# Order of the last two blocks, gather rate, return of inputs and a table load in a hybrid block with PEER

## The chip, the cores and the metric

The kernel runs on 1 core of one Trainium2 chip. The metric is the device time of one execution in microseconds (us), 2298.05 as the median of 3 runs of the kernel before (2295.23 to 2303.24).

## The reference

One layer, 256 tokens of width 2048, all in float32. A modulated RMS norm of x feeds one projection w_in, whose columns go to a spatial-gating MLP and to a retention of 8 heads; two gated projections of these are added, multiplied by w_o, scaled by a gate and added to x. Then comes PEER: from the second normed and modulated h2, 8 heads choose 16 of 128 x 128 experts per token; each expert has a row u and a row v of 2048 values. What is computed in the part that matters here:

```
a = einsum('td,thkd->thk', xt, emb_u[it])
w = gelu(a) * gate
y = einsum('thk,thkd->td', w, emb_v[it])
x = x + ga2 * y
out = rmsnorm(x, norm_f_g)
```

## The kernel before, in words

The program is one long list of instructions, written with a planner that gives each engine its order: of what is ready by its own model it takes first what stands first in the program, and adds the semaphore waits. A tile pool with n buffers makes the next writer wait until the last reader of that buffer is done.

The stages up to PEER's choice are jobs, each a weight matrix streamed in 1 MB tiles on SP's queue, split into a high and a low part (ScalarE casts the high part, line 213; VectorE subtracts, line 215), and multiplied on TensorE (line 414). The w_o jobs are the last before the second norm. After each of their eight 256-column pieces, `wo_post` (line 661) adds the result to x, takes sums of squares on ScalarE (line 675) and stores x1 to device memory. `norm2` (line 715) then reduces the sums, takes reciprocal and square root (`rsqrt`, lines 169 to 172) and starts the choice of experts on TensorE behind `prs` (line 723).

The last stage computes y. Columns 0 to 575 of each chosen row of peer_v are gathered, one DMA for each of 256 (token half, choice) pairs (`fly`, line 1100, issued by GpSimd at line 757 and spread over the products), and VectorE weighs and adds them into yg (`weigh`, line 1103). The other 1472 columns come as a product: all weights stand in a table A of 128 x 128 experts per token, and each of NK = 128 blocks multiplies a 128 x 256 slice of A by 128 rows of peer_v. `v_load` (line 1116) loads a block's rows vb on SP's queue (three buffers), casts the slice to wh and vb to vh on ScalarE, and subtracts to wl and vl on VectorE (two buffers each). A block is 18 products, (wh, vh), (wl, vh), (wh, vl) for 2 token halves and 3 chunks of 512, 512 and 448 columns. All six sums stay in PSUM through the stage.

The loop (line 1184) runs over blocks 0 to 125. After the products of a block it issues gathers at `rate` per block, 256 / (NK - ENDS), weighs all but BEHIND = 4 of those in flight, and after block BACK it calls `restore`, which loads ga2, x1 and norm_f_g (four loads of 1024 KB) into a part of A that is no longer read. Each of these loads waits for the last product of that block. The two last blocks are multiplied after the loop, one token half at a time; each half ends in `finish` (line 1160): `residual` multiplies a chunk by ga2, adds x1 and squares (the gathered columns' part on GpSimd and ScalarE), then the sums are reduced, the root is taken, the chunks are scaled and stored. The residual's first multiplication also waits for the last vl.

Of the kernel before, what the change touches and what calls it, by code (L numbers as in the profile page):

```python
# [10 lines left out]
F32 = mybir.dt.float32  # L11
# [11 lines left out]
P = 128  # L23
T = 256
TT = T // P
# [8 lines left out]
NK = 128  # L34
# [26 lines left out]
FK = KD - UK  # L61
GW = 576
ON_POOL = ((0, 3), (1, 3))
BACK, ENDS = NK - 5, 4
VG, BEHIND, BEHIND_U = 7, 4, 2
COLS = 2 * NK - 50
GV = D - GW
# [49 lines left out]
def block_kernel(ctx, tc, a, out):  # L117
    nc = tc.nc
    def pool(name, side, bufs=1, space=None):
        stack = ExitStack()  # L120
        kw = {} if space == bass.MemoryType.DRAM else {"reuse_waits": "tile"}
        if space is not None:
            kw["space"] = space
        return stack.enter_context(tc.tile_pool(name=name, bufs=bufs, side=side, **kw)), stack
# [5 lines left out]
    late = {}  # L130
# [3 lines left out]
    sb, sb_s = pool("p1", "left")  # L134
# [5 lines left out]
    def bank(name):  # L140
        return late["side"].tile([P, 512], F32, tag="side", name=name)
# [32 lines left out]
    ss = sb.tile([P, TT], F32, name="ss")  # L174
# [486 lines left out]
    def wo_post(c, off=0):  # L661
        def post(ps):
            c0 = c * GC
            if c == 0:
                late["x1T"] = st.tile([P, KD, T], F32, tag="A16", name="x1T")
                late["ss"] = sb.tile([P, TT, 8], F32, name="ss2")
            ga, gg = late["ga"][:, off:off + GC], late["gg"][:, off:off + GC]
            xc = st.tile([P, TT, GC], F32, tag="tmp_a", name="xc")
            nc.sync.dma_start(xc, xv[:, :, c0:c0 + GC])
            mx = st.tile([P, TT, GC], F32, tag="tmp_c", name="mx")  # L670
            for tt in range(TT):
                nc.vector.tensor_tensor(mx[:, tt], ps[tt], ga, op=ALU.mult)
            nc.vector.tensor_tensor(xc, xc, mx, op=ALU.add)
            for tt in range(TT):
                nc.scalar.activation(mx[:, tt], xc[:, tt], AF.Square, accum_out=late["ss"][:, tt, c:c + 1])
            nc.sync.dma_start(x1d[:, :, c0:c0 + GC], xc)
            if c0 >= UG:
                hr = st.tile([P, TT, GC], F32, tag="tmp_d", name="x1g")
            else:
                hr = h2b[:, :, c0:c0 + GC]  # L680
            nc.vector.tensor_tensor(hr, xc, gg[:, None, :].to_broadcast([P, TT, GC]), op=ALU.mult)
            if c < 7:
                yield
            pt = bank("pt")
            ptv = pt.rearrange("p (k t) -> p k t", k=2)
            for k in range(2):
                for tt in range(TT):
                    nc.tensor.transpose(ptv[:, k, tt * P:(tt + 1) * P], hr[:, tt, k * P:(k + 1) * P], ident)
            nc.scalar.copy(late["x1T"][:, 2 * c:2 * c + 2], ptv)
        return post  # L690
# [374 lines left out]
    for u in range(-LEAD, units + LAG):  # L1065
        if 0 <= u < units and u % half == 0:
            tt = u // half
# [45 lines left out]
    chunks = [(c, min(512, GV - c)) for c in range(0, GV, 512)]  # L1113
    yp = [[py.tile([P, 512], F32, name=f"yp{tt}_{c}") for c, _ in chunks] for tt in range(TT)]

    def v_load(i):
        room, bufs = (p3, 1) if i % 3 == 2 else (pv, 2)
        vb = room.tile([P, GV], F32, tag="vb", bufs=bufs, name="vb")
        nc.sync.dma_start(vb, v_cols[i * P:(i + 1) * P])
        wh = p3.tile([P, T], F32R, tag="wh", bufs=3, name="wh")  # L1120
        w = of_key(i)
        nc.scalar.copy(wh.rearrange("p (g s) -> p g s", s=2), w)  # L1122
        wl = p3.tile([P, T], F32R, tag="wl", bufs=3, name="wl")
        nc.vector.tensor_tensor(wl.rearrange("p (g s) -> p g s", s=2), w, wh.bitcast(F32).rearrange("p (g s) -> p g s", s=2), op=ALU.subtract)  # L1124
        vh = p3.tile([P, GV], F32R, tag="vh", bufs=2, name="vh")
        nc.scalar.copy(vh, vb)  # L1126
        vl = p3.tile([P, GV], F32R, tag="vl", bufs=2, name="vl")
        late["split"] = nc.vector.tensor_tensor(vl, vb, vh.bitcast(F32), op=ALU.subtract)  # L1128
        return vh, vl, wh, wl
# [30 lines left out]
    def finish(tt):  # L1160
        for m in range(len(chunks)):
            residual(tt, m)
        r = rf[:, tt:tt + 1]
        nc.vector.tensor_reduce(r, ss3[:, tt], axis=AX.X, op=ALU.add)
        rsqrt(r, r, 1.0 / D)
        for c, w, n in parts:
            xs = xo[:, tt, c:c + w]
            if n is None:
                nc.scalar.activation(xs, xs, AF.Copy, scale=r)
            else:  # L1170
                nc.vector.scalar_tensor_tensor(xs, xs, r, gf[:, c:c + w], op0=ALU.mult, op1=ALU.mult)  # L1171
            nc.sync.dma_start(ov[:, tt, c:c + w], xs)

    def product(i, ops, j, tt, n):
        vh, vl, wh, wl = ops
        l, r = ((wh, vh), (wl, vh), (wh, vl))[j]
        c, w = chunks[n]
        return nc.tensor.matmul(yp[tt][n][:, :w], l[:, tt * P:(tt + 1) * P], r[:, c:c + w],  # L1178
                                start=(i == 0 and j == 0), stop=(i == NK - 1 and j == 2))
# [4 lines left out]
    for i in range(NK - 2):  # L1184
        ops = nxt
# [12 lines left out]
    ends = [nxt, v_load(NK - 1)]  # L1198
# [2 lines left out]
    for tt in range(TT):  # L1201
        residual(tt, len(parts) - 1)
    for tt in range(TT):
        for j in range(3):
            for n in range(len(chunks)):
                product(NK - 2, ends[0], j, tt, n)
        for n in range(len(chunks)):
            for j in range(3):
                product(NK - 1, ends[1], j, tt, n)
        finish(tt)  # L1210
    big_s.close()
    p3_s.close()
# [52 lines left out]
```

## Time and profile before

| | |
|---|---|
| median of the runs | 2298.05 us |
| profiled execution: its own time, span | 2299.92 us, 2298.1 us |
| mean granted TensorE clock | 0.980 |
| busy, share of span: TensorE, VectorE, ScalarE, GpSimd | 93%, 78%, 43%, 41% |
| read from device memory, mean rate | 631.59 MB, 278 GB/s |
| last stage's first product, last product, end | 1745.6, 2279.1, 2298.1 us |

PE is TensorE's products, PEld its weight loads, DVE VectorE, ACT ScalarE, POOL GpSimd, SP the queue of most loads; L1178 is line 1178. In a timeline a line has start and length in us, engine, line, operation, output<-input, count, and in brackets the idle time before it and what ended that. A line of windows has the stretch, its length, the busy us (and count) of PE, PEld, DVE, ACT and POOL, the granted clock, the busy share of the DMA engines and what they moved in GB/s. A group has busy us and mean ns, then the idle us before its instructions and what ended them.

### The profile page before, as it was taken

The page shows a single profiled execution, that of the slowest core. Times are in us where ns is not written, and L with a number is a line of the kernel's source. Part 1 is how long each engine was busy: PE and PEld are TensorE (multiplying, and loading weights), DVE is VectorE, ACT ScalarE, POOL GpSimd, SP SyncE. Part 2 cuts the span into 40 slices and gives each one's busy share as a digit, 9 for nine tenths or more (in the row PEclk, how much of TensorE's full clock was granted, in tenths as well). Part 3 has the DMA queues.
Part 4 walks back from the last instruction along what each step waited for, and adds up shares of the span by engine and source line. Part 5 has one row for each costly group of instructions (what it writes and reads, how often), then busy time and mean ns, then how long its engine had stood idle before and what let it go on. Part 6 is the DMA issues. An engine that isn't in the chain of part 4 may idle for free. (4 is left out here: it accounts for less than half of the span.)

```text
span 2298.1 us, 37147 instructions
## 1 busy us (share of the span) xinstructions
PE 2145.9 (93%) x13918; PEld 1921.9 (84%) x13918; DVE 1792.4 (78%) x3402; ACT 999.1 (43%) x1426; POOL 941.3 (41%) x750
## 2 busy tenths in 40 slices
PE   5999999999999998989699999997889999999996
PEld 3678888999999977978599999997888878888785
DVE  3469888888889855688677777778997788888887
ACT  3235556553344445110234444446775444444443
POOL 0000000000000001566634444447896888888784
PEclk9999999999999999999899999998999999999998
DMA  8987777788878866658999999994105999999997
GB/s 337 378 313 268 286 280 280 278 288 292 297 280 296 312 206 216 232 180 276 313 301 321 327 319 322 315 318 128 60 2 187 325 327 336 338 322 331 319 327 272
DMA packets 144311, 638.25 MB, mean 278 GB/s; under 512 B 20721, under 2 KB 26625, under 8 KB 112001
## 3 DMA queue, kind: packets, MB, share of 16 engines
q1 hardware_dynamic: 102146, 459.65, 56.1%
q0 software_dynamic: 41984, 176.23, 22.3%
q8 instruction: 109, 1.79, 0.3%
q14 instruction: 72, 0.59, 0.1%
HBM read 631.59 MB, written 4.20 MB: 277 GB/s over the span
## 5 line engine op out<-in xcount | busy, mean ns | idle before, releaser
L757 POOL DMA_INDIRECT gat<-in_peer_v_rows,eidx x256 | 416.0, 1625 | 106.8 <-issue 38.0
L757 POOL DMA_INDIRECT gat<-in_peer_u_rows,eidx x256 | 312.2, 1220 | 281.7 <-PE mmu L900 178.2
L213 ACT CAST whi<-wt 128x2048 fp32r<-128x2048 f32 x130 | 248.1, 1909 | 280.1 <-PE mm L414 210.1
L764 DVE SCALAR_TENSOR_TENSOR gat<-gat,h2b 128x768 f32<-128x768 f32 x256 | 250.3, 980 | 112.3 <-DMA gat<-in_peer_u_rows,eidx 105.8
L215 DVE TENSOR_TENSOR wlo<-wt,whi 128x2048 fp32r<-128x2048 f32 (+1 forms) x130 | 292.3, 2249 | 52.7 <-ACT whi L213 49.1
L358 POOL DMA_DIRECT2D br<-in_b_ada x32 | 15.8, 495 | 764.7 <-DVE ada_acc L359 719.1
L900 PE MATMUL mmu<-h2T,uhi 128*128 128x256 f32 x2220 | 308.8, 287 | 11.1 <-ACT uhi L711 11.1
L1126 ACT CAST vh<-vb 128x1472 fp32r<-128x1472 f32 x128 | 183.1, 1430 | 300.0 <-DMA vb<-in_peer_v_cols 195.1
L711 ACT CAST uhi<-ub 128x640 fp32r<-128x640 f32 x222 | 161.0, 728 | 317.7 <-DMA ub<-in_peer_u_cols 258.1
L900 PEld LDWEIGHTS mmu<-h2T,uhi 128*128 128x128 f32 x2220 | 285.8, 194 | 15.5 <-ACT uhi L711 15.1
L1109 DVE SCALAR_TENSOR_TENSOR yg<-gat,wrow,yg 128x576 f32<-128x576 f32 x254 | 207.6, 817 | 77.6 <-DMA gat<-in_peer_v_rows,eidx 74.5
L355 DVE SCALAR_TENSOR_TENSOR ada_acc<-wa,sc_col,ada_acc 128x256 f32<-128x256 f32 x480 | 231.8, 483 | 11.5
L1128 DVE TENSOR_TENSOR vl<-vb,vh 128x1472 fp32r<-128x1472 f32 x128 | 215.7, 1685 | 10.4 <-ACT vh L1126 10.4
L1178 PE MATMUL yp<-vl,wh 128*128 128x512 f32 (+1 forms) x768 | 195.5, 389 | 13.7 <-DVE vl L1128 13.4
L900 PE MATMUL mmu<-h2T,ulo 128*128 128x256 f32 x1110 | 175.2, 289 | 24.8 <-DVE ulo L712 22.6
L1178 PE MATMUL yp<-vh,wh 128*128 128x512 f32 (+1 forms) x768 | 192.5, 385 | 3.0 <-ACT wh L1122 2.3
L712 DVE TENSOR_TENSOR ulo<-ub,uhi 128x640 fp32r<-128x640 f32 x222 | 180.4, 823 | 17.5 <-ACT uhi L711 14.1
L1178 PE MATMUL yp<-vh,wl 128*128 128x512 f32 (+1 forms) x768 | 192.6, 385 | 0.0
L1178 PEld LDWEIGHTS yp<-vl,wh 128*128 128x128 f32 x768 | 142.8, 189 | 48.2 <-DVE vl L1128 22.8
L414 PE MATMUL mm<-whi,hT 128*128 128x512 f32 (+1 forms) x832 | 181.8, 363 | 0.0
L900 PEld LDWEIGHTS mmu<-h2T,ulo 128*128 128x128 f32 x1110 | 150.8, 194 | 31.5 <-DVE ulo L712 27.1
L1178 PEld LDWEIGHTS yp<-vh,wh 128*128 128x128 f32 x768 | 144.9, 189 | 28.8 <-ACT wh L1122 2.5
(276 smaller groups left out, 3662.7 us busy)
## 6 DMA issues: line engine op xcount, KB each, us to landing
wa<-in_w_ada SPq DMA_DIRECT2D x96, 1024.0 KB
vb<-in_peer_v_cols SPq DMA_DIRECT2D x128, 736.0 KB
ub<-in_peer_u_cols SPq DMA_DIRECT2D x256, 320.0 KB
wt<-in_w_vg SPq DMA_DIRECT2D x32, 1024.0 KB
wt<-in_w_branch_gate SPq DMA_DIRECT2D x32, 1024.0 KB
wt<-in_w_u SPq DMA_DIRECT2D x16, 1024.0 KB
wt<-in_w_b_out SPq DMA_DIRECT2D x16, 1024.0 KB
wt<-in_w_o SPq DMA_DIRECT2D x16, 1024.0 KB
```

The lines of the kernel that those rows point to most:

```text
L213: nc.scalar.copy(hi, wt)
L215: nc.vector.tensor_tensor(lo[:, :cut], wt[:, :cut], hi[:, :cut].bitcast(F32), op=ALU.subtract)
L355: nc.vector.scalar_tensor_tensor(acc, wt[:, k], s, acc, op0=ALU.mult, op1=ALU.add)
L414: nc.tensor.matmul(job.ps[b], l, r, start=(first and k == 0 and i == 0 and not lo_part), stop=(last and k == job.rows - 1 and lo_part == 1))
L712: late["lo"] = (nc.gpsimd if n < POOL else nc.vector).tensor_tensor(lo[:, :w], ub[:, :w], hi[:, :w].bitcast(F32), op=ALU.subtract)
L757: d = nc.gpsimd.indirect_dma_start(out=g, out_offset=None, in_=table, in_offset=bass.IndirectOffsetOnAxis(ap=rows_of("idx")[:, tt, n:n + 1 ...
L764: return nc.vector.scalar_tensor_tensor(g, g, 1.0, h2b[:, tt, :UG], op0=ALU.mult, op1=ALU.mult, accum_out=pe["wrow"][:, tt, n:n + 1])
L900: mm = nc.tensor.matmul(acc, w[:, k - k0], x, start=(first and k == 0 and i == 0), stop=(last and k == FK - 1 and i == len(steps) - 1))
L1109: d = nc.vector.scalar_tensor_tensor(yg[:, tt], g, w, yg[:, tt], op0=ALU.mult, op1=ALU.add)
L1126: nc.scalar.copy(vh, vb)
L1128: late["split"] = nc.vector.tensor_tensor(vl, vb, vh.bitcast(F32), op=ALU.subtract)
L1178: return nc.tensor.matmul(yp[tt][n][:, :w], l[:, tt * P:(tt + 1) * P], r[:, c:c + w], start=(i == 0 and j == 0), stop=(i == NK - 1 and j = ...
```

## The change

Four edits. BACK goes from block 123 to block 112, ENDS from 4 to 7. In the w_o stage a square root of one column of the sums, whose result nothing reads, is taken after the third piece. The two last blocks are multiplied chunk by chunk: of a chunk first block 126's three products, then block 127's.

```diff
-BACK, ENDS = NK - 5, 4
+BACK, ENDS = NK - 16, 7
@@ wo_post
+            if c == 2:
+                warm = sb.tile([P, TT], F32, name="warm")
+                nc.scalar.sqrt(warm, late["ss"][:, :, 0])
@@ after the loop
     for tt in range(TT):
-        for j in range(3):
-            for n in range(len(chunks)):
-                product(NK - 2, ends[0], j, tt, n)
         for n in range(len(chunks)):
-            for j in range(3):
-                product(NK - 1, ends[1], j, tt, n)
+            for i, ops in enumerate(ends):
+                for j in range(3):
+                    product(NK - 2 + i, ops, j, tt, n)
         finish(tt)
```

## Rows read from the trace of the kernel before

**Rows 1.** Chain that ended last, in order of time (start, length, what), end of run.
```profile
2265.08 14.71 DMA A<-in_norm_f_g
```
**Rows 2.** Windows: a stretch of the last stage, and the loads' last stretch.
```profile
2160.00:2200.00 40.00, 40.00 (x184) 34.10 (x183) 33.44 (x39) 16.25 (x21) 29.49 (x20) 1.00 0.92 317
2264.00:2278.00 14.00, 12.34 (x55) 9.88 (x54) 11.36 (x14) 3.95 (x5) 1.70 (x1) 1.00 0.99 397
```
**Rows 3.** Timeline, TensorE in the last stage: idle places, and products after one.
```profile
1745.58 1.83 PE L1178 MATMUL yp<-vh,wh 128*128 128x512 f32 x6 [2.31 <-ACT wh L1122]
...
1819.17 1.60 PE L1178 MATMUL yp<-vl,wh 128*128 128x512 f32 x6 [1.14 <-DVE vl L1128]
...
2143.95 2.82 PE L1178 MATMUL yp<-vl,wh 128*128 128x512 f32 x6 [3.48 <-DVE vl L1128]
2146.57 2.65 PE L1178 MATMUL yp<-vh,wh 128*128 128x512 f32 x6
...
2150.62 1.48 PE L1178 MATMUL yp<-vl,wh 128*128 128x512 f32 x6
...
2211.23 1.60 PE L1178 MATMUL yp<-vl,wh 128*128 128x512 f32 x6 [0.80 <-DVE vl L1128]
...
2235.63 1.60 PE L1178 MATMUL yp<-vl,wh 128*128 128x512 f32 x6 [0.37 <-DVE vl L1128]
```
**Rows 4.** Groups of GpSimd and VectorE, 1760 to 2260 us.
```profile
L757 POOL DMA_INDIRECT gat<-in_peer_v_rows,eidx x249 | 407.9, 1638 | 93.3 <-issue 36.4 <-PE yp L1178 24.1 <-DVE wl L1124 22.4
L1128 DVE TENSOR_TENSOR vl<-vb,vh 128x1472 fp32r<-128x1472 f32 x121 | 203.9, 1685 | 0.7 <-ACT vh L1126 0.7
L1109 DVE SCALAR_TENSOR_TENSOR yg<-gat,wrow,yg 128x576 f32<-128x576 f32 x247 | 201.4, 815 | 76.4 <-DMA gat<-in_peer_v_rows,eidx 73.3 <-issue 2.4
```
**Rows 5.** Timeline, loads on SP, casts of vb, TensorE's last block.
```profile
2186.46 1.43 ACT L1126 CAST vh<-vb 128x1472 fp32r<-128x1472 f32 x1 [2.22 <-PE yp L1178]
...
2263.20 0.33 SPq L1119 DMA_DIRECT2D vb<-in_peer_v_cols  x1
2263.58 0.43 SPq L1142 DMA_DIRECT2D A<-ga2d  x1
...
2270.11 1.42 ACT L1126 CAST vh<-vb 128x1472 fp32r<-128x1472 f32 x1 [2.52 <-DMA vb<-in_peer_v_cols]
2271.59 0.50 PE L1178 MATMUL yp<-vh,wh 128*128 128x512 f32 x1 [0.67 <-ACT vh L1126]
...
2273.32 0.50 PE L1178 MATMUL yp<-vl,wh 128*128 128x512 f32 x1 [0.99 <-DVE vl L1128]
...
2278.73 0.36 PE L1178 MATMUL yp<-vl,wh 128*128 128x448 f32 x1
```
**Rows 6.** Timeline, VectorE in the last 27 us.
```profile
2271.57 1.69 DVE L1128 TENSOR_TENSOR vl<-vb,vh 128x1472 fp32r<-128x1472 f32 x1 [2.23 <-ACT vh L1126]
...
2281.56 2.49 DVE L1155 TENSOR_TENSOR A<-A 128x448 f32<-128x448 f32 x2
...
2286.55 0.16 DVE L1164 TENSOR_REDUCE rf<-ss 128x1 f32<-128x4 f32 x1 [1.90 <-ACT A L1156]
...
2291.57 2.01 DVE L1171 SCALAR_TENSOR_TENSOR A<-A,rf 128x512 f32<-128x512 f32 x3 [0.27 <-ACT rf L172]
```
**Rows 7.** Timeline, a gap of ScalarE in the w_o stage; then norm2.
```profile
850.84 1.91 ACT L213 CAST whi<-wt 128x2048 fp32r<-128x2048 f32 x1 [2.62 <-issue]
...
905.33 1.09 PE L688 MATMUL pt<-kst,x1g 128*128 128x128 f32 x4 [5.64 <-DVE x1g L681]
905.48 1.28 ACT L172 ACT_TABLE_LOAD   x1
...
905.90 0.17 DVE L171 RECIPROCAL ssum<-ssum 128x2 f32<-128x2 f32 x1
...
906.77 0.20 ACT L172 ACTIVATE ssum<-ssum 128x2 f32<-128x2 f32 x1
...
907.03 1.22 PE L723 MATMUL prs<-kst,ssum 128*128 128x128 f32 x4 [0.61 <-ACT ssum L172]
```

## The prediction

> **What bounds the kernel now.** I read the chain of waits first, for the end of the run: its last long link before the finish is the transfer of norm_f_g, from 2265.08 to 2279.8 us, for which GpSimd waits with its work on the output [rows 1]. The last product ends at 2278.73 + 0.36 = 2279.1 us [rows 5]; the span ends at 2298.1. So 19.0 us pass after TensorE has done its last work, and edits to the end compete for those 19. The windows came second: in the stage of peer_v, TensorE is busy for all of a 40 us stretch while the DMA engines are busy for 92% of it [rows 2]. Third, TensorE's own idle places there: the largest of some 17 between 1760 and 2265 us are waits for vl, the low half of an operand that VectorE computes [rows 3]. Fourth, the groups of GpSimd and VectorE in 1760 to 2260: the 249 gathers of that stretch cost GpSimd 407.9 us of busy time and 36.4 us of fixed idle time, and VectorE waits 73.3 us for gathered rows that it weighs, in order, ahead of the next vl [rows 4]. So three things run close to full beside TensorE: transfers, gather issue, VectorE's order. A block of 18 products takes 3 x 1.32 = 3.96 us when nothing waits (the groups of six follow each other by 1.32 us); 128 of them are 507 us, and the stage takes 2279.1 - 1745.6 [rows 3] = 533.5.
>
> **The square root's table.** In norm2 the table load runs from 905.48 to 906.77, the square root follows at once, and its reader on TensorE starts at 907.03 [rows 7]. The reciprocal ends at 905.90 + 0.17 = 906.07, and TensorE's transposes ahead of that reader end at 905.33 + 1.09 = 906.42. With the table there, the reader starts at 906.42 instead of 907.03: -0.6 us. The added pair in the w_o stage is a load of 1.28 and an operation of 0.20 on ScalarE; it reads sums of squares that are long there. It is hidden by ScalarE's waits in that stage, 2.62 us in the one shown [rows 7]. If it falls just ahead of a split cast instead, the cast and TensorE behind it can be late by 1.5. Range -0.6 to +1.5; I take -0.6, since later squares and copies run under the same table (the final stage does so with only one load).
> The Trainium skill (ScalarE: Activation LUTs, section What ACT_TABLE_LOAD costs) gives the load the same 1283 ns but adds a drain of about 1380 ns per switch. Here no such drain shows: the operation stands directly behind the load [rows 7]. By the page this edit would give about -2.0 and the sum would be 1.4 us lower.
>
> **Gathers end 7 blocks ahead.** The rate goes from 256/124 = 2.065 to 256/121 = 2.116 gathers a block. By the loop's rule a block issues three gathers, not two, at blocks 0, 15, 31, 46, 62, 77, 93 and 108 now, and at 14 blocks then: six more. Three blocks behind each of the seven later ones TensorE waits for vl: 1.14 us at 1819.17, 3.48 at 2143.95, 0.80 at 2211.23 [rows 3], and between these 0.87, 0.76, 0.77 and 1.05; the median is 0.87. After the wait of 3.48 the clock also fell to half: six products begun at 2146.57 took 2.65 instead of 1.48 us [rows 3], and the 18 from 2143.95 ended 2.6 later than at full clock. Six more waits at 0.87 are 5.2; the three further blocks without gathers give back some 0.2 each, and some of the small waits would merge. I take +4. Bounds: -1 (waits come from elsewhere) to +10 (each as dear as the mean, 1.27, plus its share of clock loss). GpSimd leaves little room: (407.9 + 36.4) / 249 = 1.78 us a gather, 3.77 a block at 2.116, of 3.96.
>
> **The inputs return at block 112.** restore issues four transfers of 1024 KB, 4.19 MB, on SP's queue. Now they stand behind the last vb load (2263.20, then 2263.58) [rows 5], when gathers have all but ended: nothing but the tail waits for them. Then they stand between the loads of blocks 116 and 117, with gathers still flowing until block 120. Queued behind them on SP are the vb loads of all later blocks, and behind those vh, vl and the products. At the rate of the stretch in which they run now, 397 GB/s [rows 2], they take 10.6 us. Against that stand: the 8% of DMA time that is free, 1 us over the 12 us that loaded operands last; and the lead that a load has where nothing waits. A load lands 6.9 us after issue (2263.20 to 2270.11 [rows 5]) and is wanted three blocks less about 1.3 us after it, 10.6, so the lead is up to 3.7. That leaves a TensorE wait of 6 us at block 117, and one such wait costs the clock as at 2143.95: +2.6. The waits that this stretch has now go: 0.37 at 2235.63 [rows 3] and 0.67 + 0.99 for the last block's vh and vl [rows 5], -2.0. Net +6.6. Bounds: a wait of 0 (DMA engines take it beside the rest) to 11 (no lead).
>
> **The last two blocks, chunk by chunk.** The same 36 products, 7.9 us. With today's arrival of vl the new order would wait earlier, since the first chunk needs both blocks: +1.4. But the last seven blocks carry no gathers, so vb, vh and vl of block 127 come as soon as their buffers are free, when block 125 ends; I cost this at 0. The order gives VectorE its first finished chunk 6 products into the pair.
> The tail, from TensorE's end E: now 19.0. VectorE needs from the end of its last vl (2271.57 + 1.69) to its last scaling (2291.57 + 2.01) 20.3 us [rows 6]. Of this go the last four weighings of gathered rows, 3.2 (815 ns each [rows 4]), the wait of 1.90 for squares that stood behind GpSimd's work on norm_f_g, and 1.3 by which two additions beside GpSimd took longer (2.49 for two) [rows 6]: 13.9 are left. Its last vl then ends at E - 7.9 + 1.7 = E - 6.2, so its last scaling ends at E + 7.7, and the outputs follow in 4.5 as now (2293.6 to 2298.1): E + 12.2. The tail shrinks by 6.8. Bounds: -9.4, where only the last chunk's own chain counts (multiply, add, square, root, three scalings and output, 9.6), and -4, if VectorE's order is no better.
>
> **Sum.** -0.6 + 4 + 6.6 - 6.8 = +3.2. The profiled execution took 2299.9 with a span of 2298.1, 1.9 over the median of 2298.05; from the median the forecast is **2301 us**. What is won in the tail is spent ahead of it.
>
> **Rivals.** First, the return is hidden: with the lead, and large packets for which the DMA engines go up to 397 GB/s where they otherwise stand near 317 [rows 2], no vb load is late. For it: there are stretches, from 2150 to 2191 all of one, in which each vh waits for TensorE and not for a landing; the cast at 2186.46 stands for 11 [rows 5]. Against: at 2270.11 a load lands too late even with few gathers [rows 5]. Then -0.6 + 1.5 (gathers, near their lower bound) + 0 - 2.0 - 8 (tail, between its bounds) = -9: 2289.
> Second, on the slower side: the return blocks the queue in full. Gathers keep taking their part of the engines while TensorE uses up blocks 113 to 116, so the load of block 117 lands 11 us late, whatever lead there was, and the denser gathers cost 6: -0.6 + 6 + 11 + 2.6 - 2.0 - 6.8 = +10: 2308. It decides from a TensorE wait of over 9 us at block 117. The busy share of 92% speaks for it, the stretches without any landing wait against it.
> The Trainium skill (DMA: Bandwidth & Descriptors, Queues, rings and completion order) says that each DMA engine takes turns between the queues with work, a packet at a time, and serves one queue in order; by that the gathers, on GpSimd's queue, pass the returned inputs while the vb loads, on SP's, cannot. That is this second rival, and no row here has both at once.
> Third, the change doesn't do what it says: the planner puts the return later in SP's order, or the residual's first part late in VectorE's, and the tail stays: -0.6 + 4 - 1 = +2: 2300.
>
> **How the numbers follow.** Forecast case 0.36, hidden 0.34, blocked 0.26, third 0.04. What a measurement can tell from no change is 0.3%, 6.9 us: 2291.2 to 2304.9. The forecast case gives same 0.28, faster 0.04, slower 0.04; hidden gives faster 0.30, same 0.04; blocked slower 0.23, same 0.03; the third same. Faster 0.34, same 0.39, slower 0.27. The cases of both signs weigh much, so the range is wide, 2288 to 2311; the forecast's own is 2295 to 2307.
>
> **What would show it.** A TensorE wait of some 6 us near block 117 (about 2235 us), with half clock behind it; more waits for vl, three blocks behind each block with three gathers; no table load in norm2 and one near 840; no wait on norm_f_g in the last 20 us; last product to end of span about 12 us. No wait at block 117 makes me wrong towards 2289; a tail that stays near 19 makes me wrong the other way.

## The result, and the profile after

The changed kernel takes 2316.64 us as the median of 6 runs (2310.92 to 2317.97), beside 2300.03 for the kernel before on the same chip (6 runs): a ratio of 1.0072, 95% interval 1.0050 to 1.0093. It is slower, by 16.6 us at the median, where 2301 with a range of 2288 to 2311 was predicted. Its profiled execution took 2317.25 us with a span of 2315.4, 17.3 more than the span of before. In the two traces the difference lies here:

| stretch | before | after | difference | predicted |
|---|---|---|---|---|
| start to the last stage's first product | 1745.58 | 1745.65 | +0.1 | -0.6 |
| first product to the start of block 113 | 471.0 | 477.7 | +6.7 | +4 |
| block 113 to the end of the last product | 62.5 | 74.5 | +12.0 | +6.6 |
| last product to the end of the span | 19.0 | 17.6 | -1.4 | -6.8 |

Block 113 starts at 2216.62 before and at 2223.34 after; the last product ends at 2279.09 and 2297.85. All three large terms missed on the same side: of the 14.1 us between the 17.3 measured and the 3.2 predicted, 5.4 are the return, 5.4 the tail, 2.7 the gathers and 0.7 the table.

**The return.** TensorE's timeline of the kernel after, at the places of [rows 3], begins with two of the waits behind blocks with three gathers; the other rows are blocks 114 to 117 and the first one back at speed:

```profile
1902.14 1.60 PE L1181 MATMUL yp<-vl,wh 128*128 128x512 f32 x6 [3.01 <-DVE vl L1131]
...
2050.72 2.65 PE L1181 MATMUL yp<-vl,wh 128*128 128x512 f32 x6 [2.85 <-DVE vl L1131]
...
2230.29 1.60 PE L1181 MATMUL yp<-vl,wh 128*128 128x512 f32 x6 [0.18 <-DVE vl L1131]
...
2237.17 1.60 PE L1181 MATMUL yp<-vl,wh 128*128 128x512 f32 x6 [2.40 <-DVE vl L1131]
2238.60 2.57 PE L1181 MATMUL yp<-vh,wh 128*128 128x512 f32 x6
...
2242.82 1.50 PE L1181 MATMUL yp<-vl,wh 128*128 128x512 f32 x6
2252.26 2.82 PE L1181 MATMUL yp<-vh,wh 128*128 128x512 f32 x6 [7.94 <-ACT vh L1129]
...
2256.60 1.48 PE L1181 MATMUL yp<-vl,wh 128*128 128x512 f32 x6
```

The 7.94 is block 117's wait, at the block that the prediction named. The 2.40 is block 115's, three blocks behind a block with three gathers. After each the next 12 products run slow: from 2238.60 to 2242.82 in 4.22 us and from 2252.26 to 2256.60 in 4.34, instead of 2 x 1.32. That is 3.3 us of clock. Waits of 10.5 (2.40, 7.94 and 0.18; the last block has none), less the 2.0 that stood in this stretch before, plus 3.3 make 11.8 of the 12.0. How much of the 2.40 belongs to the inputs is not shown: with the same gathers and no inputs there (back5, below) blocks 114 and 115 have waits of 0.79 and 0.64, with the same gathers and inputs (drain) block 114 has 0.86 and block 115 none.

The SP queue and ScalarE's casts in the same stretch of the kernel after, which answer to [rows 5]:

```profile
2224.70 0.33 SPq L1122 DMA_DIRECT2D vb<-in_peer_v_cols  x1
2225.08 0.42 SPq L1145 DMA_DIRECT2D A<-ga2d  x1
...
2226.86 0.71 SPq L1145 DMA_DIRECT2D A<-in_norm_f_g  x1
...
2230.26 30.05 SPq L1122 DMA_DIRECT2D vb<-in_peer_v_cols  x6
...
2232.41 1.43 ACT L1129 CAST vh<-vb 128x1472 fp32r<-128x1472 f32 x1 [2.15 <-DMA vb<-in_peer_v_cols]
...
2250.79 1.42 ACT L1129 CAST vh<-vb 128x1472 fp32r<-128x1472 f32 x1 [6.01 <-DMA vb<-in_peer_v_cols]
```

The load of block 116's rows is issued just ahead of the four inputs and cast at 2232.41. The load of block 117 is issued at 2230.26, when its buffer comes free, some 5 us behind the inputs, and its cast starts at 2250.79: 20.5 us from issue, where [rows 5] had 6.9. The windows say what the DMA engines did meanwhile (columns as in [rows 2]):

```profile
2230.00:2235.00 5.00, 4.58 (x19) 3.22 (x18) 1.69 (x4) 2.01 (x3) 3.93 (x4) 1.00 1.01 401
2235.00:2240.00 5.00, 2.83 (x10) 2.40 (x11) 4.20 (x6) 0.42 (x1) 2.13 (x2) 0.87 1.01 416
2240.00:2245.00 5.00, 4.32 (x15) 3.22 (x14) 3.80 (x6) 0.42 (x1) 2.37 (x2) 0.79 1.02 408
2245.00:2250.00 5.00, 0.00 (x0) 0.00 (x0) 0.24 (x1) 0.00 (x0) 1.61 (x2) 0.89 1.02 406
2250.00:2255.00 5.00, 2.74 (x7) 2.27 (x8) 2.42 (x2) 2.46 (x2) 0.00 (x0) 0.50 0.78 301
```

From 2230 to 2250 they are busy without a break and move 401 to 416 GB/s, while TensorE is idle for the whole window from 2245 to 2250. In the window behind that idle time the granted clock is 0.50, the lower of its two levels (1.2 GHz). It is not the DMA engines that rest, it is the one load that TensorE needs that stands behind 4.19 MB that nobody needs yet. Nor is all that they move on SP's queue. Between issue and landing of block 117's load, 2230.26 to 2250.79, the queues had these packets, MB and shares of the DMA engines' time; q1 carries the loads on SP, q0 the gathers:

```profile
q1 hardware_dynamic: 814, 5.37, 64.5%
q0 software_dynamic: 805, 2.95, 36.7%
```

SP's queue got 5.37 MB in 20.5 us, 262 GB/s, while the gathers took over a third of the engines. The chain of waits of the kernel after has this landing as its last long link before the products that run to the end:

```profile
2228.55 1.70 DVE vl L1131
2230.26 20.51 DMA vb<-in_peer_v_cols
...
2252.26 36.20 PE yp L1181 x156
...
2296.27 1.90 DVE yg L1112
...
2299.52 1.79 POOL A L1158
```

norm_f_g, the last long link of [rows 1], is gone. In its place stands yg, line 1112: a weighing of gathered rows, in the tail.

**The tail.** VectorE in the last 27 us of the kernel after, and GpSimd's part beside it, as in [rows 6]:

```profile
2289.94 1.69 DVE L1131 TENSOR_TENSOR vl<-vb,vh 128x1472 fp32r<-128x1472 f32 x1 [1.93 <-ACT vh L1129]
2291.55 0.81 DVE L1112 SCALAR_TENSOR_TENSOR yg<-gat,wrow,yg 128x576 f32<-128x576 f32 x1
...
2292.95 0.81 DVE L1112 SCALAR_TENSOR_TENSOR yg<-gat,wrow,yg 128x576 f32<-128x576 f32 x1
...
2294.28 1.39 DVE L1112 SCALAR_TENSOR_TENSOR yg<-gat,wrow,yg 128x576 f32<-128x576 f32 x1
...
2295.94 1.62 POOL L1161 TENSOR_TENSOR A<-A 128x576 f32<-128x576 f32 x1 [0.89 <-ACT A L1159]
...
2296.19 1.98 DVE L1112 SCALAR_TENSOR_TENSOR yg<-gat,wrow,yg 128x576 f32<-128x576 f32 x1
...
2304.35 0.16 DVE L1167 TENSOR_REDUCE rf<-ss 128x1 f32<-128x4 f32 x1 [1.36 <-ACT A L1159]
...
2309.37 2.01 DVE L1174 SCALAR_TENSOR_TENSOR A<-A,rf 128x512 f32<-128x512 f32 x3 [0.27 <-ACT rf L172]
```

The last four weighings are still there, 0.81 + 0.81 + 1.39 + 1.98 = 5.0 us of VectorE, two of them slowed beside GpSimd's work. So is the wait for squares, 1.36. From the end of the last vl to the end of the span it is 23.8 us, against 24.8 before.

**The table.** In norm2, the place of [rows 7]:

```profile
903.05 0.17 DVE L171 RECIPROCAL ssum<-ssum 128x2 f32<-128x2 f32 x1
903.25 0.20 ACT L172 ACTIVATE ssum<-ssum 128x2 f32<-128x2 f32 x1 [0.64 <-DVE ssum L171]
903.50 1.22 PE L726 MATMUL prs<-kst,ssum 128*128 128x128 f32 x4
```

From the reciprocal's start to `prs` it is 0.45 us, 1.13 before [rows 7]: -0.68. The load now runs at 819.80 for 1.28 us.

### The profile page after: what moved, and what is told of

Read it like the earlier page. It is cut to its first block, busy times and chain, and to the rows that moved or that the text cites. A ratio compares the mean times of both kernels' runs of the same rounds, so it can differ in the third digit from the quotient of the medians.

```text
span 2315.4 us, 37140 instructions
## 1 busy us (share of the span) xinstructions
PE 2153.4 (93%) x13918; PEld 1924.6 (83%) x13918; DVE 1790.1 (77%) x3402; ACT 999.6 (43%) x1427; POOL 931.3 (40%) x750
## 5 line engine op out<-in xcount | busy, mean ns | idle before, releaser
L760 POOL DMA_INDIRECT gat<-in_peer_v_rows,eidx x256 | 405.1, 1582 | 127.8 <-PE yp L1181 46.5
L903 PEld LDWEIGHTS mmu<-h2T,uhi 128*128 128x128 f32 x2220 | 285.9, 194 | 13.5 <-ACT uhi L714 12.8
L355 DVE SCALAR_TENSOR_TENSOR ada_acc<-wa,sc_col,ada_acc 128x256 f32<-128x256 f32 x480 | 231.8, 483 | 11.5
L1181 PE MATMUL yp<-vh,wh 128*128 128x512 f32 (+1 forms) x768 | 195.8, 389 | 10.3 <-ACT vh L1129 7.9
```

The lines of the kernel that those rows point to most:

```text
L355: nc.vector.scalar_tensor_tensor(acc, wt[:, k], s, acc, op0=ALU.mult, op1=ALU.add)
L760: d = nc.gpsimd.indirect_dma_start(out=g, out_offset=None, in_=table, in_offset=bass.IndirectOffsetOnAxis(ap=rows_of("idx")[:, tt, n:n + 1 ...
L903: mm = nc.tensor.matmul(acc, w[:, k - k0], x, start=(first and k == 0 and i == 0), stop=(last and k == FK - 1 and i == len(steps) - 1))
```

## The experiments

Ten kernels. "To 113" is first product to the start of block 113, "113 to end" from there to the end of the last product, "tail" the rest of the span, each from one profiled execution. The ratios are against the kernel before in runs on the same chip (6 to 12 runs of each kernel, 6 to 34 of the one before). The kernel before had a median of 2300.03 beside after, 2297.25 beside back5 to spread and 2295.46 beside the two early ones, so kernels are compared by their ratios, not by their medians.

| kernel | median us | ratio, 95% | to 113 | 113 to end | tail |
|---|---|---|---|---|---|
| before | 2300.03 | | 471.0 | 62.5 | 19.0 |
| after | 2316.64 | 1.0072 (1.0050 to 1.0093) | 477.7 | 74.5 | 17.6 |
| back5 | 2299.87 | 1.0014 (1.0000 to 1.0028) | 472.3 | 62.1 | 18.0 |
| ends4 | 2304.67 | 1.0025 (1.0005 to 1.0046) | 466.3 | 76.0 | 17.6 |
| pool_queue | 2305.44 | 1.0034 (1.0013 to 1.0056) | 477.6 | 67.3 | 18.2 |
| drain | 2309.28 | 1.0056 (1.0040 to 1.0073) | 479.6 | 75.9 | 14.1 |
| order_warm | 2295.97 | 0.9998 (0.9981 to 1.0015) | 467.3 | 65.2 | 18.0 |
| back16 | 2306.42 | 1.0040 (1.0025 to 1.0056) | 470.9 | 71.7 | 17.8 |
| ends7 | 2301.66 | 1.0015 (0.9999 to 1.0031) | 475.5 | 61.5 | 18.2 |
| spread | 2295.24 | 0.9982 (0.9966 to 0.9997) | 467.1 | 65.2 | 14.1 |
| early | 2291.67 | 0.9973 (0.9957 to 0.9989) | 459.5 | 63.1 | 14.2 |
| early_late_return | 2288.23 | 0.9965 (0.9950 to 0.9980) | 460.1 | 64.9 | 13.0 |

The first product itself starts between 1737.9 and 1752.5 in these executions, so spans of single profiles scatter by far more than the stretches do.

### Without the early return (back5)

```diff
-BACK, ENDS = NK - 16, 7
+BACK, ENDS = NK - 5, 7
```

> The changed kernel with BACK = NK - 5, ENDS = 7 and the rest as changed. Theory (the four returned inputs stand ahead of the vb loads on SP's queue, while gathers still flow): the waits of TensorE at blocks 115 to 117 (2.40 and 7.94 us) and the half clock behind them go, 12 us less from block 113 to the last product; the tail stays about 18 us, since the inputs land late again; about 2305 us. Rival (the waits there come from the denser gathers, and the return only meets them): a wait of several us stays between blocks 110 and 120, 2312 or more.

The stretch from block 113 took 62.1 us, 12.4 less than after, and the median is level with before to within 0.3%. With the other edits in place and the inputs late, the stretch is as short as before: the return accounts for the whole 12. By the ratios, 1.0072 to 1.0014, it is 13 us. The total came out some 5 us under what was expected.

### Without the denser gathers (ends4)

```diff
-BACK, ENDS = NK - 16, 7
+BACK, ENDS = NK - 16, 4
```

> The changed kernel with ENDS = 4, BACK = NK - 16 and the rest as changed. Theory (a block with three gathers makes VectorE late with vl, and there are 14 such blocks instead of 8): the 6.7 us lost between the stage's start and block 113 go, the wait at block 117 stays; about 2310 us. Rival (the loss before block 113 is scatter between executions, or has another cause): block 113 starts as late as in the changed kernel, 2316 us.

The stretch to block 113 took 466.3, 11.4 less than after where 6.7 was expected (executions scatter by some 3 us here), but the return cost as much as there (76.0). TensorE's wait at block 117 and the cast that it waits for:

```profile
2241.73 1.42 ACT L1129 CAST vh<-vb 128x1472 fp32r<-128x1472 f32 x1 [12.31 <-DMA vb<-in_peer_v_cols]
...
2243.20 2.82 PE L1181 MATMUL yp<-vh,wh 128*128 128x512 f32 x6 [14.23 <-ACT vh L1129]
```

The wait is 14.23, not 7.94: here nothing held TensorE at block 115, so it came to block 117 sooner and waited there for a landing as late. The size of one wait is a poor measure; the landing is the thing.

### The inputs on GpSimd's queue (pool_queue)

```diff
-            return nc.sync.dma_start(dst, bass.AP(...))
+            return nc.gpsimd.dma_start(dst, bass.AP(...))
...
-        loads += [nc.sync.dma_start(x1[:, tt], x1d[:, tt]) for tt in range(TT)]
+        loads += [nc.gpsimd.dma_start(x1[:, tt], x1d[:, tt]) for tt in range(TT)]
```

> The changed kernel with the four returned inputs issued by GpSimd instead of SP, after the same block. Theory (the vb loads wait in order behind them on SP's queue): vb loads pass, the wait at block 117 falls under 3 us, about 2307 us. Rival (the transfers as a whole are short of time, whichever queue carries them): the wait stays at 7 us or more, or is split over vb loads and gathers, 2314 or more.

Same bytes, same blocks, another queue. The time of issue moved too: GpSimd comes to the inputs at 2231.14, 7 us after the start of block 113, where SP had issued them 2 us after it. Block 117's load still stands behind the first three of them in time of issue. Its issue and cast, and the three of TensorE's waits in that stretch that are over 1 us:

```profile
2232.73 24.71 SPq L1122 DMA_DIRECT2D vb<-in_peer_v_cols  x6
...
2242.75 1.42 ACT L1129 CAST vh<-vb 128x1472 fp32r<-128x1472 f32 x1 [7.93 <-DMA vb<-in_peer_v_cols]
...
2232.76 1.60 PE L1181 MATMUL yp<-vl,wh 128*128 128x512 f32 x6 [1.98 <-DVE vl L1131]
...
2244.22 1.60 PE L1181 MATMUL yp<-vh,wh 128*128 128x512 f32 x6 [1.94 <-ACT vh L1129]
...
2257.15 1.60 PE L1181 MATMUL yp<-vl,wh 128*128 128x512 f32 x6 [1.41 <-DVE vl L1131]
```

The products behind them keep their speed. The load is cast 10.0 us after issue instead of 20.5, while the four inputs land 7.1 to 18.3 us after theirs: on another queue it lands ahead of the last two of them, one of which was issued before it. 113 to end is 67.3: 7.2 of the 12.4 us go with the inputs off SP's queue (and issued later), 5.2 (against back5) are left: vb loads and gathers lose a share of the transfers, and GpSimd has four more issues. How these two divide was not tried.

### The last weighings ahead of the tail (drain)

```diff
+        if todo:
+            emptied = i + 1
-        while len(flying) > BEHIND:
+        while len(flying) > max(0, BEHIND - 2 * (i - emptied if not todo else 0)):
             weigh()
```

> The changed kernel, with the last four weighings of gathered rows done in blocks 121 and 122 instead of behind the last vl. Theory (these four, tied behind the last vl, and GpSimd's and ScalarE's work behind them hold the tail at 17.5 us): the tail shrinks by 4 to 5 us, 2312 us. Rival (the tail is set by the last products and the additions, which wait for TensorE): the tail stays above 16.5, 2316 us.

Once no gathers are left to issue, the four in flight are weighed within the next blocks. The tail is 14.1, 3.5 less than after where 4 to 5 were expected; VectorE at the end of this kernel (span 2307.5), and GpSimd's part beside it:

```profile
2285.46 1.69 DVE L1131 TENSOR_TENSOR vl<-vb,vh 128x1472 fp32r<-128x1472 f32 x1 [1.93 <-ACT vh L1129]
...
2289.73 2.57 DVE L1158 TENSOR_TENSOR A<-A 128x512 f32<-128x512 f32 x2
...
2291.71 3.62 POOL L1161 TENSOR_TENSOR A<-A 128x576 f32<-128x576 f32 x2
...
2293.35 2.53 DVE L1158 TENSOR_TENSOR A<-A 128x448 f32<-128x448 f32 x2
...
2296.41 0.14 DVE L1167 TENSOR_REDUCE rf<-ss 128x1 f32<-128x4 f32 x1
```

The sum of the first half's squares waits for nothing now. From the end of the last vl to the end of the span it is 20.3 us, against 23.8 after. The predicted term for the tail needed this, and the change did not contain it. What is left over the predicted 12.2 are mostly the four additions shown, 5.1 us beside GpSimd's work where they take some 2.5 alone.

### Chunk order and table load alone (order_warm), early return alone (back16), denser gathers alone (ends7)

```diff
-BACK, ENDS = NK - 16, 7      # of the changed kernel: order_warm
+BACK, ENDS = NK - 5, 4
...
-BACK, ENDS = NK - 5, 4       # of the kernel before: back16
+BACK, ENDS = NK - 16, 4
...
-BACK, ENDS = NK - 5, 4       # of the kernel before: ends7
+BACK, ENDS = NK - 5, 7
```

> The kernel before with the chunk-by-chunk order and the early table load alone (BACK = NK - 5, ENDS = 4). Theory (neither is on the path that sets the end): within 2 us of the kernel before; the last products wait up to 1.4 us longer, since vl of block 127 lands late; norm2 is 0.6 us shorter and what follows takes it back. Rival (the order is what holds the tail): the tail changes by more than 2 us either way.

> The kernel before with BACK = NK - 16 alone. Theory (the vb load of block 117 stands behind 4.19 MB on SP's queue): TensorE waits 10 to 14 us for vh near block 117, with 2.6 us of half clock behind, the tail falls by 1.5 to 2, about 2308 us. Rival (only together with the denser gathers is there a wait): no wait over 4 us there, 2298 or less.

> The kernel before with ENDS = 7 alone. Theory (14 blocks with three gathers, each late with vl, and VectorE, GpSimd and transfers all near full): block 113 starts 6 to 9 us later after the stage's start than in the kernel before; the waits for the last block go, -1.7; the tail keeps its 18 us; about 2303 us. Rival (the cost is scatter): block 113 within 2 us, 2296.

order_warm measures no change: 1 us off the tail, 2.7 more from block 113 on. In its trace the first chunk asks for block 127 six products earlier than the old order did, and block 127 is not there:

```profile
2275.90 0.51 PE L1181 MATMUL yp<-vh,wh 128*128 128x512 f32 x1 [1.91 <-ACT vh L1129]
...
2276.63 0.63 PE L1181 MATMUL yp<-vh,wh 128*128 128x512 f32 x1
```

After it a product takes 0.63 instead of 0.39. back16 costs 9.2 us in its stretch and 0.4% in the median, with its own wait for the landing at block 117, just under the 10 to 14 expected:

```profile
2242.44 2.82 PE L1178 MATMUL yp<-vh,wh 128*128 128x512 f32 x6 [9.26 <-ACT vh L1126]
```

ends7 costs 4.5 us up to block 113, less than the 6 to 9 expected, and its interval for the whole just reaches 1. Medians of the parts, -0.5 + 9.2 + 3.4 by their ratios, make 12 against 16.6 for all together (interval 11.5 to 21.4): near enough that no interaction has to be claimed.

### The inputs one at a time (spread)

```diff
-BACK, ENDS = NK - 16, 7
+BACK, ENDS = (54, 70, 85, 101), 4
...
-        if i == BACK:
-            restore(mm)
+        if i in BACK:
+            restore(mm, BACK.index(i))
```

> The changed kernel with ENDS = 4, the last weighings done two blocks after the last gather, and the four returned inputs loaded one at a time, after blocks 54, 70, 85 and 101. Theory (one load of 1 MB, 2.6 us, fits in the lead of the vb loads, up to 3.7 us): no wait over 2 us behind these blocks, the tail 14 us; about 2294 us. Rival (transfers are full in this stage, so 4.19 MB cost 10 us wherever they stand): the stage is 8 to 12 us longer up to block 113, 2303 us.

`restore` issues one of its four loads a time (ga2, the halves of x1, norm_f_g), still on SP's queue, with the weighings moved as in drain. The stretch to block 113 stays at 467.1, as in order_warm (467.3), which has no load there. The largest wait that stands behind such a load is this one, five blocks later, at block 75:

```profile
2044.33 0.44 SPq L1150 DMA_DIRECT2D A<-x1d  x1
...
2060.70 1.60 PE L1181 MATMUL yp<-vh,wh 128*128 128x512 f32 x6 [1.54 <-ACT vh L1129]
```

So 1 MB in the queue is nearly all taken by the loads' lead, and 4.19 MB are not.

### Seven gathers ahead of the loop (early, early_late_return)

```diff
+    for _ in range(VG):
+        fly(*todo.pop(0), after=None)
     done, rate, emptied = 0, len(todo) / (NK - ENDS), 0
```

> The kernel of e9_spread with the first seven gathers issued ahead of the loop, so that 249 are left for 124 blocks: 2.008 a block, and one block with three (the first) instead of eight. Theory (blocks with three gathers cost the stage some 1.3 us each): block 113 starts 6 to 9 us earlier after the stage's start than in e9_spread (467), about 460; 2288 us. Rival (the waits come from the mean load, which changes by 3% only): 465 or more, 2294 us.

> The kernel of e10_early with the four returned inputs loaded together after block 123, as in the kernel before. Theory (once the last weighings are out of the tail, the late inputs hold it): the tail is 17 to 18.5 us instead of 14, so 3 to 4 us over e10_early. Rival (the tail is set by VectorE's own work, and the inputs come in time): tail within 1 us of e10_early's, the same total.

early is spread with seven gathers issued before block 0; 249 then go over 124 blocks, with one block of three gathers instead of eight. early_late_return is the same with the four inputs together after block 123 again (`BACK, ENDS = NK - 5, 4`). Up to block 113 both take about 460 us, the tail is 14.2 and 13.0, and early_late_return has the lowest ratio of all: 0.9965 of the kernel before (0.9950 to 0.9980). It beats both kernels; that it beats early or spread is not shown, their intervals overlap. By the ratios early gains only 0.09% on spread, 2 us, where its one profile is 7.6 us ahead at block 113. The tail of early_late_return (span 2280.5), with the inputs landing as late as before the change:

```profile
2258.39 1.69 DVE L1131 TENSOR_TENSOR vl<-vb,vh 128x1472 fp32r<-128x1472 f32 x1 [1.00 <-ACT vh L1129]
...
2266.92 2.78 POOL L1161 TENSOR_TENSOR A<-A 128x576 f32<-128x576 f32 x2 [1.03 <-DMA A<-in_norm_f_g]
...
2273.96 2.01 DVE L1174 SCALAR_TENSOR_TENSOR A<-A,rf 128x512 f32<-128x512 f32 x3 [0.27 <-ACT rf L172]
```

GpSimd waits for norm_f_g here as in [rows 1], by 1.03 us. The theory that the late inputs would hold the tail at 17 to 18.5 fails; its rival comes out, to 1.2 us. That the tail is the shortest is no gain of its own: TensorE ends later behind the last vl here (7.4 us, 6.2 in early), since the pair of last blocks takes 13.2 us with its waits (11.6 in early, 8.2 in back5). From the end of the last vl to the end of the span it is 20.4 us, and 20.3 in drain, spread and early, whose inputs land long ahead; with the weighings in the tail it is 23.8 to 24.4 with early inputs (after, ends4, back16, pool_queue) and 24.2 to 25.5 with late ones (before, back5, ends7, order_warm). So the late inputs cost up to 1.7 us while the weighings stood there and nothing once they were moved; what held the end was VectorE's order.

## Why the prediction was wrong, step by step

**The return (+6.6 predicted, 9 to 12 measured by the stretches, 6 to 13 by the ratios).** The mechanism was right, a wait for a late landing at block 117; two terms of its sum failed. The first is "At the rate of the stretch in which they run now, 397 GB/s [rows 2], they take 10.6 us", less 1 us of free DMA time: that rate belongs to a stretch where gathers have all but ended. Here the gathers took 2.95 MB of the 8.3 that moved, SP's queue ran at 262 GB/s, and the landing came 20.5 us after issue, 13.6 later than in [rows 5] instead of 9.6 (13.6 to 15.9 in after, ends4, drain and back16). The second is "so the lead is up to 3.7". Block 117's load was issued only at 2230.26, when VectorE's vl had freed its buffer; at full pace its cast was due at 2223.34 + 4 x 3.96 - 1.47 = 2237.7, 7.4 us after issue, which leaves a lead of 0.5. So it landed 13.1 us late instead of 6. In back16, where the lead was 4.0, it landed 10.0 late. That is the end of the first rival, too, by which no load would be late. The second rival, the queue blocked in full with gathers taking their part, had the mechanism. pool_queue bears it out: with the inputs on another queue, 7 of 12 us go. Its threshold, a wait of over 9 us at block 117, was badly put: after has 7.94 there, but only since 2.40 were already spent at block 115; ends4 has 14.23, drain 12.99, back16 9.26. By that, the rule of the Trainium skill (DMA: Bandwidth & Descriptors, Queues, rings and completion order) that one queue is served in order while others take turns agrees with the runs: on SP's queue the vb load stands behind the inputs, on another it landed ahead of two of the four. The clock loss came as predicted in kind, 3.3 us in two falls for 2.6 in one.

**The gathers (+4 predicted, 6.7 measured).** The mechanism was right as far as the runs tell, the size was off: the term "six more waits at 0.87". It counted the waits that stood out in [rows 3] and took their median. (Three of the seven, the 1.14 and the 3.48 among them, begin two blocks behind the block with three gathers, not three.) The runs order themselves by the number of blocks with three gathers: with 14 of them (after, back5, pool_queue, drain, ends7) the stretch to block 113 takes 476.5 us on the mean, with 8 (before, ends4, order_warm, back16, spread) 468.5, with 1 (the two early ones) 459.8. That is 8.0 / 6 = 1.33 and 8.7 / 7 = 1.24 us for each, the mean of 1.27 that the prediction had used for its upper bound, with a clock loss now and then (the 2.65 at 2050.72). Single runs scatter by 3 us either way. It also means, as an estimate, that the eight such blocks of the kernel before had cost it some 10 us. By [rows 4] three gathers take 3 x 1.78 = 5.3 us of GpSimd, 1.4 more than a block's 3.96, and a third weighing takes VectorE past a block as well; which of the two sets the wait is not shown. Nor do the runs part the blocks with three from the mean rate, for both fall together (2.116, 2.065 and 2.008 gathers a block); that the waits stand just behind those blocks speaks for the blocks.

**The tail (-6.8 predicted, -1.4 measured).** Its failed step is "of this go the last four weighings of gathered rows". They did not go, and with -1.4 the tail lies outside even the bound of -4. Ending the gathers earlier lands the rows earlier, but the loop weighs down only to BEHIND = 4 in flight, and the remaining four are weighed after the loop, and line 1110 of the kernel before puts those behind the last vl (`late["split"]`, which `v_load` of block 127 sets just before). The prediction read the order from what the rows wait for and not from the code that orders them. The last vl did end 6.2 us before the last product (2291.63 to 2297.85), as worked out; but the last scaling ended 13.5 behind the last product instead of 7.7: the weighings (5.0) and the wait for squares (1.4) were still there. With the weighings moved the tail is 14.1 (drain), against the 12.2 predicted, for one more piece of the term failed: additions beside GpSimd's work go on taking longer. The reading that opened the argument, norm_f_g as the last long link [rows 1], was a false lead: a chain names what came last, not how soon the next thing would be last without it.

**Chunk order at 0.** The alternative that the prediction set aside, +1.4 because the first chunk needs both blocks, is what order_warm shows (a wait of 1.91, with slow products behind it, in place of 0.67 and 0.99). back5, with gathers ended earlier, has 62.1 in that stretch, so there the assumption held; after, too, has no wait in the last block, and its last two blocks take 8.2 us instead of 10.3. In order_warm, early and early_late_return, whose gathers end four blocks ahead, the two blocks take 11.9, 11.6 and 13.2 us. The two early kernels were not tried with the old order.

**The table (-0.6 predicted, -0.68 at its place).** Right where it was looked for: 0.45 us from reciprocal to reader instead of 1.13. The Trainium skill (ScalarE: Activation LUTs, What ACT_TABLE_LOAD costs) adds a drain of about 1380 ns to the load, by which the prediction had -2.0; the trace has no drain (load to 906.77, square root from 906.77 [rows 7]). Whether the 0.68 us reaches the end is open, since the last stage's start scatters by up to 15 us between the executions.

## What to carry to other kernels

A prefetch moved forward on a queue that a tight loop feeds from delays the loop by the whole transfer, at the rate that this queue gets beside the others (262 GB/s here, not 397), less only the lead that its loads have at that moment; split it into pieces that the lead covers, put it on another queue, or leave it behind the loop's last load. Before a wait at the end of the chain is priced, ask what ends a microsecond earlier, and read in the code which statement ties the work that is meant to move. Where work is spread over blocks by a rate, count the blocks that get one more: six more of them cost 4.5 us (ends7) to 8 us (the means) up to block 113, and the slack that they bought gave back 2 us in the last two blocks.

## What was not expected of the hardware

With 4.19 MB of large loads among them, the DMA engines moved 401 to 416 GB/s at a busy share of 1.01 to 1.02, and with vb loads and gathers alone 335 GB/s at 0.93 (early, 2222 to 2262 us). More bytes per second did not make the needed load come sooner. VectorE's weighing of 128x576 took 0.81 us alone and 1.98 where GpSimd's work on the same size ran beside it (2296.19), more than double.
